# A Strassen step in the projections of five head pairs: 1024 columns as 2x2 blocks with seven block products in four PSUM banks

## The chip, the cores and the metric

The kernel runs on one core of one Trainium2 chip. The metric is the time of one execution on the device in microseconds, and the kernel before takes 841.94 us (median of three runs). Engines are named as the profile names them: PE is the matrix engine, with PEld for its weight loads; DVE is VectorE; ACT is ScalarE; POOL is GpSimd; SP is the engine that issues nearly all transfers.

## The reference, cut to what matters

Two layers on one sequence of 512 tokens and 1024 channels. Each normalises its input, projects it with one wide matrix, mixes tokens by attention, multiplies with a gate, projects back and adds the residual. Layer A has three groups of dilated window attention, so its projection has 10 blocks of 1024 columns: q, k and v for each of three groups, and the gate.

```python
def mixer_a(hn, w_in, w_out, q_gain, k_gain, t5_bias):
    proj = hn @ w_in                                  # (512, 1024) @ (1024, 10240)
    n_qkv = N_DIL_GROUPS * 3 * BRANCH_WIDTH
    qkv = proj[..., :n_qkv].reshape(b, s, N_DIL_GROUPS, 3, N_HEADS, HEAD_DIM)
    gate = proj[..., n_qkv:]
    for g, (window, dilation) in enumerate(DILATED_PAIRS):
        q = rms_norm(qkv[:, :, g, 0], q_gain[g])
        k = rms_norm(qkv[:, :, g, 1], k_gain[g])
        v = qkv[:, :, g, 2]
        o, lse = dilated_group_attention(q, k, v, t5_bias[...], dilation, reach)
    alpha = jax.nn.softmax(jnp.stack(lses), axis=0)
    y = jnp.sum(alpha[..., None] * jnp.stack(outs), axis=0)
    y = y.reshape(b, s, BRANCH_WIDTH) * jax.nn.silu(gate)
    return y @ w_out
```

Layer B is neighbourhood attention on an 8 x 64 grid, with a projection to 4096 columns; the change leaves its arithmetic alone. All inputs are float32.

## The kernel before, in words

**Split matmuls.** Every large product is made of three matmuls on operands that are split into a rounded part and the rest: h·h, h·l and l·h (`mm3`, L221). The normalised activations are split once, into `hn_h` and `hn_l`. Weights are split as they come: `loads` (L166) and `raws` (L175) bring 128 x 1024 tiles `wraw` by SP (three buffers), and `split` (L128) makes `wh` by a cast on ACT (L132) and `wl` by a subtraction (L138), two of five on POOL and the others on DVE. `wh` and `wl` have four buffers of 512 columns each, a ring that `splits` (L192) keeps three pieces ahead of the matmuls.

**Layer A** goes through eight pairs of heads (`main_a`, L548). A pair projects two blocks of 512 columns (`project_qk`, L451, by `project`, L251: eight k tiles, four token tiles of 128 in four PSUM banks, the activations stationary and the weights moving), and then two blocks of 128 columns, v of the first group (`v0_a`) and the gate (`gate_a`), the other way round (`project_t`, L276). The first block holds k and v of groups 1 and 2 (`rawk`, and `v12` of it), the second q of all groups and k of group 0 (`rawq`). At the eighth k tile each bank is evacuated by ACT with the token's norm as scale (L485); `squares` (L284) then squares on POOL (L288, L290) and sums by head on DVE (L291), and `head_norm` (L297) makes the inverse root and scales on DVE (L313).

**Attention of a pair** runs while the next pair is projected. `rawq` is turned in 32 x 32 blocks on DVE (L574), written to DRAM and read back (`move_q`); k of groups 1 and 2 is transposed on PE and scaled on DVE (L566). Scores come in two halves (`attn_a`, L774), with softmax on DVE and ACT in tile `p`; the weights are turned by DVE (L755) and by way of DRAM (`turner`), and `weigh` (L850) and `put_y` (L681) make the pair's rows of y, split again into `y_h` and `y_l`.

**What sets the order.** PE's order is written out: `run` (L914) takes the steps of `main`, keeps a clock of planned matmul time, and slips in a step of `side` (attention and everything else that is not projection) when its due time on that clock has come. A `yield "wait", key, delay` holds the next side step until a stamp and a delay after it; a guard in `main` forces side steps out until a stamp exists; `later_on` gives jobs a due time. The other engines are ordered by a scheduler ahead of time, except for instructions that are pinned to program order, and each works its queue in order.

Ahead of pair 0, `side` (near L1183) normalises, sums squares for the norm's scales, and loads tables.

## Time and profile before

| what | value |
|---|---|
| time, median of 3 runs | 841.94 us (841.76 to 842.17) |
| time of the profiled execution | 842.18 us |
| its span, first to last instruction | 840.4 us |
| instructions | 15567 |
| DVE, ACT, POOL busy | 515.4, 425.1, 283.5 us |
| HBM read, written | 109.11 MB, 31.12 MB |
| start of pairs 1 to 6 in the span | 64.6, 124.7, 188.6, 252.6, 316.5, 380.4 us |

Busy time counts an instruction from its start to its end, so a wait that an instruction spends after its start is counted as busy. Matmuls are pipelined: their own durations overlap, and the distance of their starts is what one costs. Rows of a group give the count, the busy time and the mean of one in nanoseconds, then the engine's idle time ahead of them and what ended it.

### The profile page before, as it was taken

The page shows a single profiled execution, that of the slowest core. Times are in us where ns is not written, and L with a number is a line of the kernel's source. Part 1 is how long each engine was busy: PE and PEld are TensorE (multiplying, and loading weights), DVE is VectorE, ACT ScalarE, POOL GpSimd, SP SyncE. Part 2 cuts the span into 40 slices and gives each one's busy share as a digit, 9 for nine tenths or more (in the row PEclk, how much of TensorE's full clock was granted, in tenths as well). Part 3 has the DMA queues.
Part 4 walks back from the last instruction along what each step waited for, and adds up shares of the span by engine and source line. Part 5 has one row for each costly group of instructions (what it writes and reads, how often), then busy time and mean ns, then how long its engine had stood idle before and what let it go on. Part 6 is the DMA issues. An engine that isn't in the chain of part 4 may idle for free.

```text
span 840.4 us, 15567 instructions
## 1 busy us (share of the span) xinstructions
PE 833.6 (99%) x5698; PEld 675.0 (80%) x5698; DVE 515.4 (61%) x1355; ACT 425.1 (51%) x893; POOL 283.5 (34%) x432
## 2 busy tenths in 40 slices
PE   9999999999999999999999999999999999999998
PEld 7788888788788788788788787888878877777787
DVE  7355684684584675575574755548456778668653
ACT  7432653553552652652653564345375465663551
POOL 3352442441441432432531341112521625235211
PEclk9999999999999999999999999999999999999999
DMA  7346468478368478387376364165236646457223
GB/s 254 112 122 189 150 194 245 164 215 260 127 186 238 143 222 245 107 228 231 111 221 184 111 195 126 56 231 183 78 98 182 180 142 182 129 151 204 102 94 132
DMA packets 64221, 141.25 MB, mean 168 GB/s; under 512 B 5648, under 2 KB 23248, under 8 KB 64144
## 3 DMA queue, kind: packets, MB, share of 16 engines
q1 hardware_dynamic: 64000, 139.99, 54.6%
q8 instruction: 45, 0.74, 0.4%
q14 instruction: 32, 0.26, 0.1%
q10 hardware_dynamic: 144, 0.26, 0.1%
HBM read 109.11 MB, written 31.12 MB: 167 GB/s over the span
## 4 chain that ended last, share of the span: by engine, by line
PE 93%; ACT 3%; DVE 2%; issue 1%; DMA 1%; POOL 0%; SPq 0%; DVEq 0%; ACTq 0%
PE acc L215 79%; PE o L215 5%; PE log L215 5%; PE tp L219 3%; ACT p L1101 1%; ACT p L679 1%; DVE hn_l L403 1%; DMA wraw<-in_w 1%; ACT wh L132 0%; DVE raw L313 0%; DVE p L1091 0%; ACT raw L485 0%; DVE pt L999 0%; DVE wl L138 0%; PE pa L215 0%
## 5 line engine op out<-in xcount | busy, mean ns | idle before, releaser
L132 ACT CAST wh<-wraw 128x512 fp32r<-128x512 f32 (+1 forms) x259 | 158.4, 613 | 288.8 <-PE acc L215 236.7
L215 PE MATMUL acc<-wh,hn_h 128*128 128x512 f32 x704 | 281.9, 401 | 1.3 <-ACT hn_h L402 0.7
L215 PE MATMUL acc<-wl,hn_h 128*128 128x512 f32 x704 | 274.1, 390 | 0.3 <-POOL wl L138 0.3
L215 PE MATMUL acc<-wh,hn_l 128*128 128x512 f32 x704 | 274.3, 390 | 0.0
L138 POOL TENSOR_TENSOR wl<-wraw,wh 128x512 fp32r<-128x512 f32 (+1 forms) x104 | 135.5, 1302 | 362.6 <-ACT wh L132 337.9
L138 DVE TENSOR_TENSOR wl<-wraw,wh 128x512 fp32r<-128x512 f32 (+1 forms) x156 | 114.2, 732 | 148.7 <-ACT wh L132 148.0
L215 PEld LDWEIGHTS acc<-wh,hn_h 128*128 128x128 f32 x704 | 132.1, 188 | 35.5 <-issue 5.6
L215 PEld LDWEIGHTS acc<-wh,hn_l 128*128 128x128 f32 x704 | 132.1, 188 | 28.6
L215 PEld LDWEIGHTS acc<-wl,hn_h 128*128 128x128 f32 x704 | 132.4, 188 | 25.9 <-POOL wl L138 0.8
L215 PE MATMUL acc<-y,wh 128*128 128x512 f32 (+1 forms) x272 | 82.4, 386 | 0.0
L215 PE MATMUL acc<-hn_h,wh 128*128 128x512 f32 x192 | 76.1, 397 | 0.8 <-ACT rawk L485 0.6
L215 PE MATMUL acc<-hn_h,wl 128*128 128x512 f32 x192 | 74.9, 390 | 0.0
L215 PE MATMUL acc<-hn_l,wh 128*128 128x512 f32 x192 | 74.8, 390 | 0.0
L679 ACT ACTIVATE p<-p,mn 128x512 f32<-128x512 f32 (+3 forms) x128 | 69.3, 585 | 0.7 <-DVE mn L678 0.2
L291 DVE TENSOR_REDUCE ss<-sq 128x4 f32<-128x256 f32 (+1 forms) x96 | 48.5, 505 | 28.1 <-POOL sq L290 18.3
L839 ACT ACTIVATE p<-p,mn 128x512 f32<-128x512 f32 (+1 forms) x64 | 44.9, 702 | 38.5 <-DVE mn L828 38.5
L755 DVE STREAM_TRANSPOSE tr<-p 128x512 f32<-128x512 f32 (+1 forms) x80 | 53.6, 684 | 9.3 <-ACT p L679 8.7
L215 PEld LDWEIGHTS acc<-y,wh 128*128 128x128 f32 x272 | 48.3, 189 | 9.6 <-issue 1.3
L215 PE MATMUL acc<-y,wl 128*128 128x512 f32 (+1 forms) x136 | 51.5, 379 | 0.0
L215 PEld LDWEIGHTS acc<-hn_h,wh 128*128 128x128 f32 x192 | 36.0, 188 | 9.2 <-ACT rawk L485 1.0
L215 PEld LDWEIGHTS acc<-hn_h,wl 128*128 128x128 f32 x192 | 36.0, 188 | 7.7
L215 PEld LDWEIGHTS acc<-hn_l,wh 128*128 128x128 f32 x192 | 36.1, 188 | 7.1
(128 smaller groups left out, 965.6 us busy)
## 6 DMA issues: line engine op xcount, KB each, us to landing
wraw<-in_w SPq DMA_DIRECT2D x119, 512.0 KB
td<-tr SPq DMA_DIRECT2D x14, 1024.0 KB
pt<-td SPq DMA_DIRECT2D x56, 256.0 KB
qd<-rawq SPq DMA_DIRECT2D x6, 1024.0 KB
qt<-qd SPq DMA_DIRECT2D x24, 256.0 KB
td<-tr SPq DMA_DIRECT2D x6, 896.0 KB
pt<-td SPq DMA_DIRECT2D x24, 224.0 KB
e<-l_d SPq DMA_DIRECT2D x32, 112.0 KB
```

Source lines behind the costliest of these rows:

```text
L132: nc.scalar.copy(h, raw)
L138: eng.tensor_sub(l, raw, h.bitcast(F32))
L215: nc.tensor.matmul(o, l, r, **kw)
L219: nc.tensor.transpose(o, i, ident)
L291: nc.vector.tensor_reduce(ss[:, i * ns : (i + 1) * ns], sq.rearrange("p (a b) -> p a b", b=64), axis=AX.X, op=ALU.add)
L403: return nc.vector.scalar_tensor_tensor(l, xk, g, h.bitcast(F32), op0=ALU.mult, op1=ALU.subtract)
L679: nc.scalar.activation(pr, pr, AF.Copy, scale=mn[:, 3:4])
L755: nc.vector.transpose(dst, src[:, :n].rearrange("p (i b k) -> p i b k", b=4, k=32))
L839: nc.scalar.activation(row, row, AF.Exp, bias=mn[:, 1:2], scale=-1.0, accum_out=mn[:, 2:3])
L1101: nc.scalar.activation(pr[:, o : o + n], pr[:, o : o + n], AF.Exp, bias=mn[:, 0:1], scale=-1.0, accum_out=mn[:, 2:3])
```

## The change

In pairs 1 to 5 the two blocks of 512 columns become one product of 2x2 blocks: tokens in two halves of 256, k in two halves of four tiles, columns in the two blocks of 512. `seven` (new) makes seven block products of 4 k tiles x 2 token tiles instead of eight. The stationary side of each is a block of hn or one of four forms (sums and differences of hn's blocks, split again), which `make_forms` makes once ahead of pair 0's bias tables, from whole hn tiles that `join` adds up on POOL. The moving side is a weight block or a sum of weight blocks: `sums` (new) brings the four blocks and adds them up in place on POOL, eight additions of 128 x 1024 a pair, and gives 14 tiles (28 pieces of 512) to the split, with a set of its own for which go to POOL. Products are accumulated in four PSUM banks in such an order that a bank is read once in the middle and once at the end: a column block's result is the sum of two readings, the first by ACT into SBUF, the second by DVE on top (`first`, `second`), or one reading.

With it go these moves. Squares of the five pairs go to ACT. The scaling of k12 goes from DVE to ACT. The copy of v's first 64 elements goes from POOL to ACT. The split of y for pairs 0 to 3 is put off to pair 6, since `y_l` of these shares memory with forms. The columns of the q block are permuted in DRAM for pairs 0 to 5. `wraw` has five buffers instead of three, and two tiles `wsum` are added; the bias tables `e0` and `e12`, `eg`, and `gt` have one buffer fewer, layer B's tiles borrowing others; `v12` has two places instead of three. Due times and guards of the side steps are set anew for the five pairs. Layer B and pairs 0, 6 and 7 compute as before.

```diff
+SEVEN = range(1, 6)
+SPLIT_LATER = range(0, 4)
...
+    def split(raw, n, to_pool=None):
...
-        to_pool = turn[0] * pool[0] % pool[1] < pool[0]
+        if to_pool is None:
+            to_pool = turn[0] * pool[0] % pool[1] < pool[0]
...
+            if hc in SEVEN:
+                yield b, None, None
+            else:
+                yield from ((b + 512 * KT * (i ^ first), 512, KT) for i in range(2))
...
+    def load(src, n, own=False):
+        if own:
+            raw = wp.tile([P, 1024], F32, tag="wsum", name="wsum", bufs=2)
+        else:
+            raw = wp.tile([P, 1024], F32, tag="wraw", name="wraw", bufs=5)
+        dst = raw[:, : src.shape[1]]
...
+        nc.sync.dma_start(dst, src)
...
+    def add(a, b):
+        nc.gpsimd.tensor_add(a, a, b)
+
+    def sums(off):
+
+        at = lambda n, k: w[:, off + 512 * (KT * n + k) : off + 512 * (KT * n + k + 2)]
+        js = range(2)
+        acc, x, y, z = {}, {}, {}, {}
+        for j in js:
+            acc[j] = load(at(0, 2 * j), 512, True)
+            yield acc[j], None, (1,) if j == 0 else ()
+        for j in js:
+            x[j] = load(at(1, 2 * j), 512)
+            yield acc[j], partial(add, acc[j], x[j]), ()
+        for j in js:
+            y[j] = load(at(1, 4 + 2 * j), 512)
+            yield acc[j], partial(add, acc[j], y[j]), ()
+        for j in js:
+            yield y[j], None, (1,) if j == 0 else ()
+        for j in js:
+            yield x[j], partial(add, x[j], y[j]), (1,)
+        for j in js:
+            z[j] = load(at(0, 4 + 2 * j), 512)
+            yield z[j], None, (1,) if j == 0 else ()
+        for j in js:
+            yield acc[j], partial(add, acc[j], z[j]), (1,) if j == 1 else ()
+
     def loads():
         for off, n, ks in blocks():
+            if n is None:
+                for raw, job, to_pool in sums(off):
+                    yield raw, 1024, 512, job, to_pool
+                continue
...
+    def ahead(source, n):
         queue = []
-        for src, cols, n in loads():
-            raw = wp.tile([P, 1024], F32, tag="wraw", name="wraw", bufs=3)
...
+        for item in source:
+            queue.append(item)
+            if len(queue) > n:
                 yield queue.pop(0)
         yield from queue
...
+    def summed():
+        for raw, cols, n, job, to_pool in ahead(loads(), 1):
+            if job:
+                job()
+            yield raw, cols, n, to_pool
+
+    def pieces():
+        for raw, cols, n, to_pool in ahead(summed(), 1):
...
+                pool = None if to_pool is None else c // step in to_pool
+                yield (*split(raw[:, c : c + step], step, pool), min(n, step))
+
+    def splits():
+        return ahead(pieces(), 3)
...
                 yield
 
+    def seven(hc):
+
+        ys, xs = ([ps_acc.tile([P, 512], F32, tag="acc", name="acc") for _ in range(2)] for _ in range(2))
+        part_of = lambda t, k0, i0: lambda k, i: t[:, k0 + k, P * (i0 + i) : P * (i0 + i) + P]
+        whole = lambda k0, i0: (part_of(hn_h, k0, i0), part_of(hn_l, k0, i0))
+        form = lambda n: tuple(part_of(t, 0, 0) for t in st["forms"][n])
+        q = wk.tile([P, 2048], F32, tag="rawq", name="rawq", bufs=1).rearrange("p (c i r) -> p c i r", c=16, i=4)
+        raw, st["v12", hc] = part(hc % 2), part(2 + hc % 2)
+        k_to = lambda i: sb(rk, 1024 * (hc % 2) + 256 * i, [[2048, 2], [1, 256]])
+        q_to = lambda i: q[:, :, i, :]
+        k_of = lambda t: t.rearrange("p (n c) -> p n c", n=2)
+        q_of = lambda t: t.rearrange("p (c r) -> p c r", c=16)
+        kss, qss = (wk.tile([P, 32], F32, tag="ss", name="ss") for _ in range(2))
+        first = lambda to, of, s, o: lambda i, t: nc.scalar.activation(
+            to(o + i), of(t), AF.Copy, scale=s[:, o + i : o + i + 1]
+        )
+        second = lambda to, of, s, o: lambda i, t: nc.vector.scalar_tensor_tensor(
+            to(o + i), of(t), s[:, o + i : o + i + 1], to(o + i), op0=ALU.mult, op1=ALU.add
+        )
+
+        def with_squares(put, of_k, o):
+            def both(i, t):
+                put(i, t)
+                if of_k:
+                    squares(raw[:, o + i, :], kss, o + i, 4, True)
+                else:
+                    squares(q[:, :, o + i, :], qss, o + i, 8, True)
+            return both
+
+        products = (
+            (xs, whole(0, 0), True, first(k_to, k_of, rs_n, 0)),
+            (ys, form(0), True, first(q_to, q_of, rs_neg, 2)),
+            (xs, form(1), False, first(q_to, q_of, rs_neg, 0)),
+            (ys, form(3), False, with_squares(second(q_to, q_of, rs_neg, 0), False, 0)),
+            (xs, form(2), False, with_squares(second(q_to, q_of, rs_neg, 2), False, 2)),
+            (ys, whole(4, 0), True, with_squares(second(k_to, k_of, rs_n, 0), True, 0)),
+            (xs, whole(4, 2), False, with_squares(first(k_to, k_of, rs_n, 2), True, 2)),
+        )
+        stamp["seven", hc, -1] = clock[0]
+        for n, (acc, stat, start, evac) in enumerate(products):
+            hls = {}
+            order = [(k, i) for k in range(4) for i in range(2)]
+            if n == 0:
+                order = [(0, 0), (1, 0), (0, 1), (1, 1)] + order[4:]
+            for k, i in order:
+                if k not in hls:
+                    chore(True)
+                    hls[k] = next(wsteps)
+                if k == 3 and i == 0 and n < 2:
+                    yield (("weighed", hc - 2), ("q", hc - 1))[n]
+                mm3(acc[i], stat[0](k, i), stat[1](k, i), *hls[k], start and k == 0, k == 3, skip_group_check=not start)
+                if k == 3:
+                    evac(i, acc[i])
+                yield
+            stamp["seven", hc, n] = clock[0]
+            if n == 4:
+                normed(q, qss, 8, "rawq", hc)
+        normed(raw, kss, 4, "rawk", hc)
...
+        if act:
+            nc.scalar.activation(wide, v, AF.Square)
+        else:
+            nc.gpsimd.tensor_mul(wide, v, v)
...
+    rk = wk.tile([P, 4096], F32, tag="rawk", name="rawk", bufs=1)
+    sx = big.tile([P, 4, 4, 256], F32R, name="sx")
+    st["yf"] = big.tile([P, 4, S], F32, name="yf")
...
+        late = 5000 if hc in SEVEN else 9000
+        head_norm(raw, ss, ns, False, late if key == "rawk" and 0 < hc < NHC - 1 else 0)
...
+        yield "gt", hc - 2
+        gt = wk.tile([P, S], F32, tag="gt", name="gt", bufs=2)
+        eg = wk.tile([P, S], F32, tag="eg", name="eg", bufs=1)
...
+        if hc in SEVEN:
+            nc.scalar.copy(vt[:, 0:64], vt[:, EXT - 64 : EXT])
...
+        stamp["pair", hc] = clock[0]
+        if hc == SEVEN[-1] + 1:
+            for n in SPLIT_LATER:
+                later_on(4000 + 7000 * n, partial(split_y, n))
+        if hc in SEVEN:
+            yield from seven(hc)
+        else:
+            yield from chain(*(parts[::-1] if hc == NHC - 1 else parts))
...
+        if hc in SEVEN:
+            yield "wait", ("pair", hc + 1), 9500
...
-            nc.vector.tensor_scalar(k12[:, g, :], tp, gk[:, g + 1 : g + 2], None, op0=ALU.mult)
+            scaled(k12[:, g, :], tp, g + 1)
...
+        yield "wait", ("rawq", hc), 13500 if hc in SEVEN else 18000 if moved(hc) else 13000 if hc < NHC - 1 else 23500
...
+            if hc + 1 in SEVEN:
+                yield "wait", ("pair", hc + 1), 12500 if hc else 17000
...
+            yield "wait", ("pair", hc + 1), 7000
...
+        if permuted and hc in SPLIT_LATER:
+            dst = st["yf"][:, hc, :].rearrange("p (x ja t) -> p t ja x", t=4, ja=8)
+            of = lambda t: t.rearrange("p (t ja x) -> p t ja x", t=4, ja=8)
+            tc.keep_in_program_order(nc.vector.tensor_mul(dst, of(gt), of(o)))
+            stamp["gt", hc] = 0
+            return
...
+    def split_y(hc):
+
+        h, l, y = st["y_h"][hc], st["y_l"][hc], st["yf"][:, hc, :]
+        pin(nc.scalar.copy(h, y))
+        pin(nc.gpsimd.tensor_sub(l, y, h.bitcast(F32)))
+        stamp["ya", hc, "y"] = 0
+
+    whole = pq.rearrange("p (k t) -> p k t", k=KT)
+    pin = tc.keep_in_program_order
+
+    def join(k):
+        pin(nc.gpsimd.tensor_add(whole[:, k, :], hn_h[:, k, :].bitcast(F32), hn_l[:, k, :].bitcast(F32)))
+
+    def make_forms():
+
+        y_h = st["y"][:, : KT * S].rearrange("p (n m k t) -> p n m k t", n=2, m=2, k=4)
+        st["forms"] = forms = [(y_h[:, n, 0], y_h[:, n, 1]) for n in range(2)] + [
+            (sx[:, 2 * n], sx[:, 2 * n + 1]) for n in range(2)
+        ]
+        a11, a21, a12, a22 = (whole[:, k : k + 4, t : t + 256] for k in (0, 4) for t in (0, 256))
+        f = wk.tile([P, 2, 4, 256], F32, tag="tr", name="form", bufs=1)
+
+        def cut(n, v):
+            h, l = forms[n]
+            pin(nc.scalar.copy(h, v))
+            pin(nc.vector.tensor_sub(l, v, h.bitcast(F32)))
+
+        def less(o, a, b):
+            pin(nc.vector.scalar_tensor_tensor(o, a, -1.0, b, op0=ALU.mult, op1=ALU.subtract))
+
+        pin(nc.gpsimd.tensor_sub(f[:, 0], a22, a21))
+        yield 1500
+        less(f[:, 1], f[:, 0], a11)
+        yield 1500
+        cut(0, f[:, 0])
+        yield 2000
+        less(f[:, 0], f[:, 1], a12)
+        yield 1500
+        cut(1, f[:, 1])
+        yield 2000
+        pin(nc.gpsimd.tensor_sub(f[:, 1], a11, a21))
+        cut(3, f[:, 0])
+        yield 2000
+        cut(2, f[:, 1])
+        yield 2000
+
...
+                    if hc + 1 in SEVEN:
+                        yield "wait", ("pair", hc + 1), (14500 if u == 0 else 25500) if hc else (19500 if u == 0 else 29000)
...
+            later_on(7000, lambda: st.__setitem__(("e", hc + 1), bias_a(hc + 1, True)))
+
+            def finish():
+                put_y(hc, weigh(), True, False)
+                stamp["weighed", hc] = 0
+
+            pending.append(finish)
...
+    def weigh_a(hc):
+        yield "wait", ("pair", hc + 1), 3200 if hc > 1 else 4800
+        pending.pop(0)()
+        yield
...
-            if hc == 1:
-                later_on(20000, lambda: st.__setitem__(("e", 1), bias_a(1, True)))
-            elif hc:
-                st["e", hc] = bias_a(hc)
...
+        join(0)
...
+            join(k)
...
+        st["y"] = big.tile([P, 12 * S], F32R, tag="y", name="y")
+        y = st["y"].rearrange("p (k t) -> p k t", t=S)
+        low = sx.rearrange("p a b c -> p (a b c)")
+        st["y_h"] = [y[:, k, :] for k in range(KT)]
+        st["y_l"] = [low[:, S * k : S * k + S] for k in range(4)] + [y[:, KT + k, :] for k in range(4)]
         yield 2500
+        yield from make_forms()
...
+        nc.gpsimd.tensor_scalar(rs_neg, rs_n, -1.0, None, op0=ALU.mult)
...
+                if hc in SEVEN:
+                    yield from chain(q_a(hc), weigh_a(hc), v_a(hc), k_a(hc))
+                else:
+                    yield from chain(k_a(hc), q_a(hc), v_a(hc))
```

In the lines left out, `y_h` and `y_l` become lists of slices, `project`'s uses of them follow, layer B takes the changed tiles, and `attn_a` takes new due times.

135 lines of the change are left out of this document (61 added, 74 removed).

## The prediction

> **What bounds the kernel now.** I read the page's first part, the chain of waits in order of time, PE's own waits, and then busy time pair by pair.
>
> ```profile
> span 840.4 us, 15567 instructions
> ...
> PE 833.6 (99%) x5698; PEld 675.0 (80%) x5698; DVE 515.4 (61%) x1355; ACT 425.1 (51%) x893; POOL 283.5 (34%) x432
> ```
> ```profile
> 302.56 23.17 PE acc L215 x102
> ```
> ```profile
> PE acc L215 <- ACT hn_h L402: 0.7, 1, 0.7
> ```
> TensorE is busy for all but some 7 us. The second row is one piece of the chain: 102 projection matmuls in 23.17 us with nothing between them, 0.2272 us each from start to start. The third is PE's longest wait inside the work. So the time is the number of 128x512 matmuls, as long as the other engines keep up. The profiled execution took 842.18 us, 1.8 us more than its span and 0.2 us above the median of 841.94.
>
> The next view cuts the five pairs that change into windows (start of one pair to start of the next); columns are the window's length and each engine's busy time. The last row is the same for projection matmuls alone in one of them.
>
> ```profile
> core 0: us, PE busy (x) PEld busy (x) DVE busy (x) ACT busy (x) POOL busy (x), PEclk, DMA share, GB/s
> 64.60:124.70 60.10, 60.10 (x445) 49.27 (x444) 37.80 (x100) 30.57 (x60) 22.02 (x35) 1.00 0.60 180
> 124.70:188.60 63.90, 63.90 (x493) 51.99 (x492) 39.55 (x97) 31.67 (x61) 25.25 (x40) 1.00 0.69 206
> 188.60:252.60 64.00, 64.00 (x494) 52.02 (x494) 39.06 (x99) 32.02 (x61) 22.87 (x36) 1.00 0.59 189
> 252.60:316.50 63.90, 63.90 (x493) 51.98 (x492) 39.69 (x99) 31.65 (x61) 22.77 (x36) 1.00 0.68 200
> 316.50:380.40 63.90, 63.90 (x493) 52.00 (x492) 39.90 (x99) 31.90 (x61) 22.75 (x36) 1.00 0.66 193
> sum 315.80, PE 315.80 PEld 257.26 DVE 196.01 ACT 157.81 POOL 115.66; mean PE 63.16 PEld 51.45 DVE 39.20 ACT 31.56 POOL 23.13
> ```
> A pair takes 63.16 us, all of it PE; in it DVE works 39.20, ACT 31.56 and POOL 23.13 us. The clock is 1.00 throughout.
>
> **TensorE: what is removed.** A pair's 1024 columns cost 2 blocks x 8 k x 4 token tiles x 3 = 192 matmuls. Seven products of 4 k x 2 tiles x 3 cost 168. 24 x 0.2272 = 5.45 us a pair, 27.3 us in five pairs. If nothing else is late, a pair takes 63.16 - 5.45 = 57.71 us.
>
> The Trainium skill, page "TensorE: Matmul & The Clock Gate", section "Back-to-back issue gap", gives some 131 ns for a 128x512 matmul in a sustained stream of weight loads and matmuls, and so speaks for a smaller gain: 120 x 0.131 = 15.7 us by its figure, an estimate. The trace's 0.2272 us is for the same thing, and decides.
>
> **The other engines' bill.** Rows by form (count | busy, mean ns), then the split line alone in the five pairs (min/median/max):
>
> ```profile
> L132 ACT CAST wh<-wraw 128x512 fp32r<-128x512 f32 x243 | 150.2, 619 | 272.5 <-PE acc L215 222.2 <-DMA wraw<-in_w 29.7 <-issue 6.0
> L288 POOL TENSOR_TENSOR sq<-rawq 128x512 f32<-128x512 f32 x24 | 25.5, 1083 | 6.3 <-ACT rawq L485 5.1 <-issue 1.3
> L485 ACT ACTIVATE rawq<-acc,rs_n 128x512 f32<-128x512 f32 x32 | 21.7, 688 | 0.4
> L485 ACT ACTIVATE rawk<-acc,rs_n 128x256 f32<-128x256 f32 x56 | 21.2, 489 | 0.3
> L290 POOL TENSOR_TENSOR sq<-rawk 128x256 f32<-128x256 f32 x32 | 19.5, 613 | 17.8 <-ACT rawk L485 16.5
> L566 DVE TENSOR_SCALAR k<-tp,gk 128x512 f32<-128x512 f32 x16 | 11.5, 730 | 1.1 <-PE tp L219 1.1
> L138 POOL TENSOR_TENSOR wl<-wraw,wh 128x384 fp32r<-128x384 f32 x7 | 7.1, 1014 | 45.5 <-ACT wh L132 45.5
> L1056 DVE SCALAR_TENSOR_TENSOR qkb<-tp,gk,qkb 128x512 fp32r<-128x512 f32 x8 | 6.0, 752 | 11.2 <-ACT qkb L652 11.2
> L652 ACT ACTIVATE qkb<-tp,gk 128x512 fp32r<-128x512 f32 x8 | 5.5, 685 | 5.3 <-PE tp L219 5.3
> ```
> ```profile
> L138 DVE TENSOR_TENSOR wl<-wraw,wh x60: 646/684/1509, 67.8 to 376.0; 128x512 fp32r<-128x512 f32 x60
> ...
> L138 POOL TENSOR_TENSOR wl<-wraw,wh x40: 1282/1289/1649, 68.5 to 378.6; 128x512 fp32r<-128x512 f32 x40
> ```
>
> *Splits.* Each weight piece is cast by ACT (wh) and its rest (wl) made by DVE or POOL. Today a pair has 20 pieces, 12 on DVE and 8 on POOL. Seven products need 28 pieces instead of 16, and the diff puts 6 of these on POOL; with the 4 pieces of v0 and gate (two in five on POOL) that is 24.4 on DVE, 7.6 on POOL, 32 on ACT. DVE +12.4 x 0.684 = +8.48; ACT +12 x 0.619 = +7.43; POOL -0.4 x 1.289 = -0.5 us.
>
> *Evacuation.* Today 4 of 0.688 and 8 of 0.489 on ACT, 6.66 us. Then 8 on ACT, 5.50 us, and 6 `scalar_tensor_tensor` from PSUM on DVE. Nearest row is L1056, also from PSUM with a second SBUF operand, 0.752: +4.51 us.
>
> *Squares* leave POOL (4 x 1.083 + 4 x 0.613 = 6.78) for ACT; no row shows them there, but 4 x 0.688 + 4 x 0.489 = 4.71 us, the rows of the same shapes. The two k scalings leave DVE (-1.46) for ACT (+1.37).
>
> *Sums.* Eight 128x1024 additions a pair on POOL. From 384 to 512 elements L138 on POOL grows by (1.289 - 1.014)/128 = 2.15 ns an element, which gives 2.39 us at 1024; from 256 to 512 the squares grow by 1.84 ns, which gives 2.02. I take 2.39, from the row with two different inputs: +19.1 us.
>
> Per pair: ACT 31.56 + 7.43 - 1.16 + 4.71 + 1.37 = 43.9; POOL 23.13 - 0.5 - 6.78 + 19.1 = 34.9; DVE 39.20 + 8.48 + 4.51 - 1.46 = 50.7, all under 57.7. By busy time alone PE stays the bound, with DVE at 88%.
>
> **What busy time leaves out.** Two stretches, DVE's instructions and then POOL's beside them (start, duration):
>
> ```profile
> 307.82 0.69 DVE L291 TENSOR_REDUCE ss<-sq 128x8 f32<-128x512 f32 x1 [0.31 <-POOL sq L288]
> 309.20 1.40 DVE L138 TENSOR_TENSOR wl<-wraw,wh 128x512 fp32r<-128x512 f32 x1 [0.69 <-ACT wh L132]
> ...
> 314.30 0.19 DVE L120 SCALAR_TENSOR_TENSOR rs<-na,rs 128x32 f32<-128x32 f32 x1
> ...
> 314.75 1.27 DVE L119 SCALAR_TENSOR_TENSOR na<-na,nv 128x32 f32<-128x32 f32 x1
> ```
> ```profile
> 307.75 1.30 POOL L138 TENSOR_TENSOR wl<-wraw,wh 128x512 fp32r<-128x512 f32 x1
> 309.00 1.05 POOL L288 TENSOR_TENSOR sq<-rawq 128x512 f32<-128x512 f32 x1
> ...
> 314.68 1.29 POOL L138 TENSOR_TENSOR wl<-wraw,wh 128x512 fp32r<-128x512 f32 x1 [1.81 <-ACT wh L132]
> ```
> A DVE instruction with two SBUF operands that starts while POOL reads SBUF lasts until POOL is done, and its own time more: 1.40 for 0.684, 1.27 for 0.19. The reduction at 307.82, with one operand, is not held. The delay was 0.72 of a 1.05 us instruction and 1.08 of a 1.29. The median split took 0.684, so most are spared today. The sums are nearly twice as long, eight a pair, and each stands between the split of the block it overwrites and the split of what it makes, just where DVE wants to split the other half. Bounds: none delays DVE (0), or each holds it in full, 8 x 2.39 = 19.1 us. I take half, 1.2 us each, between the splits spared and the two held: 9.6 us. DVE then needs 50.7 + 9.6 = 60.3 us, more than PE's 57.7, and the pair takes 60.3: 2.6 us given back, 13.0 in five pairs.
>
> **Start, queues, buffers.** The forms of hn (8 sums, 2 differences on POOL; 6 more steps on DVE and 4 casts) are made in pair 0:
>
> ```profile
> 0.00:64.60 64.60, 62.64 (x277) 50.37 (x278) 36.86 (x77) 33.45 (x62) 25.19 (x41) 1.00 0.50 163
> ```
> Each other engine idles 27 us or more there. 8 x 1.289 + 2 x 2.39 = 15.1 us on POOL and 6 x (2 x 0.684) = 8.2 on DVE fit; the steps push the bias tables' and the scales' matmuls back by 12.5 us of planned time, against a guard on the scales in the second block's last k. Between 0 and 2 us; I take 1.0.
>
> ```profile
> ACT wh L132 <- PE acc L215: 236.7, 128, 4.4
> ```
> ```profile
> SPq L184 <- DVE wl L138: 301.2, 81, 11.8
> ```
> Casts wait for PE to free a ring buffer and weight loads for splits, so loads (as many and as large as before) have slack: 0. But `z`'s second load waits on SP for `x`'s split, and the transfers of attention stand behind it in the queue. PSUM's four banks leave a product 24 x 0.2272 = 5.45 us until its bank is written again; two evacuations of 0.752 fit unless DVE is over 3.9 us late, and then PE stops. The deferred splits of y go to pair 6, and the single bias buffers rely on loads issued after the previous pair's last scores: 0 each, and a landing per pair if that cover fails.
>
> Sum: 842.2 - 27.3 + 13.0 + 1.0 = 828.9; 0.2 less for the median, **828.7 us**.
>
> **Rivals.**
> (1) *The sums hold DVE for most of their length.* For: both held instructions lost 0.72/1.05 and 1.08/1.29, 76% on average; DVE's queue is in order, so a held split also holds softmax and evacuations. Against: the median split is spared. At 76%, 14.5 us, DVE needs 65.2: 2.0 more than today's 63.16 in each pair, 842.2 + 10.2 + 1.0 - 0.2 = 853.2, slower. It decides from (63.16 - 50.7)/8 = 1.56 us a sum, 65%.
> The Trainium skill, page "SBUF — State Buffer", section "Who interferes with whom", states it as a rule: a Vector instruction with two SBUF inputs and a GpSimd one that reads SBUF take one shared read port exclusively, and the later fully blocks. The two held rows agree, and so does the reduction that was not.
> (2) *The sums hide.* If the queue's order puts single-operand work beside them, PE alone sets the pair: 842.2 - 27.3 + 1.0 - 0.2 = 815.7.
> (3) *The ring is too short.* Four pieces fed PE for 4 x 12 x 0.2272 = 10.9 us; now 5.45.
> ```profile
> 252.60:316.50 63.90, 0.00 (x0) 0.00 (x0) 11.43 (x24) 10.88 (x24) 0.53 (x4) 1.00 0.68 200
> ```
> This is the windows view for tile p: softmax holds DVE for 11.43 us a pair, 5.7 in each half. If a half goes ahead of the 4 splits due in it, 5.7 + 4 x 0.684 - 5.45 = 3.0 us of PE are lost. With hidden sums that is 815.7 + 15 = 830.7 for one half a pair, 845.7 for both.
>
> **Chances.** Forecast 0.45, (1) 0.28, (2) 0.15, (3) 0.12. About 0.2% (1.7 us) is what a measurement here can tell. Faster: 0.45 + 0.15 + half of (3), 0.66; same: 0.02 each from (1) and (3) at their edges, 0.04; slower: 0.26 + 0.04 = 0.30. The range goes from (2), 815, to a little past (1), 856. The forecast's own, with sums holding DVE for 40% to 60% of their length (7.6 to 11.5 us a pair), is 819 to 838.
>
> **What would show it.** Block matmuls fall from 704 to 664 in each of the three rows of acc, those named for the forms counted in; DVE busy in a pair near 60 of 60 us with splits well above 684; POOL 35; sums at 2.0 to 2.4 us; PE waits on wl, some 2 to 3 us a pair. Splits near 684 and pairs of 57.7 mean (2); PE dry behind softmax means (3); pairs over 63.2 with splits of 1.4 and more mean (1). It is also wrong if evacuations in two steps, the forms or an SP transfer stop PE for more than a microsecond a pair.

## The result: slower, 897.3 against 842.0 us

The changed kernel takes 897.33 us (median of 4 runs, 895.89 to 900.33), the kernel before 842.0 us on the same chip: ratio 1.0662, 95% interval 1.0635 to 1.0689. The forecast was 828.7. The profiled execution took 897.23 us. The page's span and its first part:

```profile
span 895.4 us, 15558 instructions
...
PE 839.4 (94%) x5578; PEld 665.6 (74%) x5578; DVE 617.3 (69%) x1437; ACT 481.7 (54%) x998; POOL 370.0 (41%) x436
```

PE runs 120 matmuls less and is busy 5.8 us longer; it was busy 99% of the span and is now at 94%. The windows of pairs 0 to 6, each from its first projection matmul to the next pair's, to within 0.2 us:

```profile
core 0: us, PE busy (x) PEld busy (x) DVE busy (x) ACT busy (x) POOL busy (x), PEclk, DMA share, GB/s
0.00:73.90 73.90, 66.87 (x272) 53.16 (x273) 53.07 (x73) 37.19 (x67) 49.89 (x54) 0.95 0.46 160
73.90:147.50 73.60, 61.75 (x420) 47.96 (x418) 59.81 (x126) 40.79 (x79) 32.64 (x33) 0.91 0.50 154
147.50:219.30 71.80, 62.94 (x469) 48.90 (x468) 57.41 (x115) 41.26 (x79) 32.48 (x28) 0.95 0.68 195
219.30:287.90 68.60, 62.47 (x470) 48.38 (x469) 54.47 (x112) 40.33 (x77) 31.64 (x31) 0.98 0.52 155
287.90:359.60 71.70, 63.93 (x469) 48.98 (x468) 58.55 (x117) 41.02 (x80) 36.48 (x37) 0.95 0.59 178
359.60:432.40 72.80, 65.18 (x470) 50.17 (x469) 56.09 (x115) 42.07 (x81) 35.30 (x39) 0.93 0.55 164
432.40:494.30 61.90, 59.74 (x478) 48.20 (x477) 30.12 (x79) 34.52 (x67) 29.27 (x44) 1.00 0.53 164
```

Pair 0 grew from 64.6 to 73.9 us, pairs 1 to 5 from 315.8 to 358.5, pair 6 from 58.5 to 61.9; what follows is 0.4 shorter. That is the whole difference of 55.0 us in span. In pairs 1 to 5 the window less PE's busy time is 42.2 us; it was zero. The granted clock, 1.00 in every one of them before, is 0.91 to 0.98: one minus the clock times the length adds up to 20.3 us. The stretches at half clock last 41.0 us, and PE stands still in 6.5 of them, so some 3 of the 20.3 are among the stops already. The 70.0 us between 27.3 saved and 42.7 lost are then 42.2 of stopped PE, some 17 of half clock while PE works, and a rest of some 11 in which matmuls start further apart, which the view counts as busy. No engine is full: DVE works 57.3 us of a mean 71.7, where the forecast had it at 60.3 of 60.3.

PE's waits, whole span (the longest of before inside the work was 0.7 us):

```profile
PE acc L265 <- DVE wl L141: 13.0, 9, 4.1
PE o L265 <- DMA pt<-td: 12.0, 4, 5.3
PE acc L265 <- POOL wl L141: 7.0, 17, 0.9
PE tp L269 <- DVE rawk L427: 6.3, 3, 3.6
PE acc L265 <- ACT rawq L601: 5.7, 2, 5.5
PE acc L265 <- ACT wh L134: 3.8, 3, 3.0
```

Not one cause: weights split late (rows 1, 3, 6), attention's transfers late (2), k late (4), and in pair 0 an evacuation that stood in ACT's queue (5). The groups that the forecast sized:

```profile
L141 DVE TENSOR_TENSOR wl<-wraw,wh 128x512 fp32r<-128x512 f32 (+1 forms) x148 | 112.2, 764 | 93.4 <-ACT wh L134 93.0
L141 DVE TENSOR_TENSOR wl<-wsum,wh 128x512 fp32r<-128x512 f32 x70 | 72.6, 1056 | 35.0 <-ACT wh L134 35.0
L190 POOL TENSOR_TENSOR wsum<-wsum,wraw 128x1024 f32<-128x1024 f32 x30 | 74.3, 2475 | 53.9 <-DVE wl L141 30.0
```

Splits of summed weights take 1.056 us in the mean against 0.764 for the others. Two stretches of pair 3, POOL's and then DVE's beside it (start, duration, and in brackets the idle time before):

```profile
216.86 2.40 POOL L190 TENSOR_TENSOR wsum<-wsum,wraw 128x1024 f32<-128x1024 f32 x1
219.22 0.65 POOL L125 TENSOR_SCALAR na<-na 128x16 f32<-128x16 f32 x1
219.84 2.39 POOL L190 TENSOR_TENSOR wraw<-wraw 128x1024 f32<-128x1024 f32 x1
222.20 0.66 POOL L126 TENSOR_TENSOR rs<-rs,na 128x16 f32<-128x16 f32 x1
222.86 2.77 POOL L190 TENSOR_TENSOR wsum<-wsum,wraw 128x1024 f32<-128x1024 f32 x1
225.59 0.40 POOL L119 TENSOR_TENSOR na<-rs 128x16 f32<-128x16 f32 x1
```
```profile
220.22 2.56 DVE L141 TENSOR_TENSOR wl<-wsum,wh 128x512 fp32r<-128x512 f32 x1 [0.41 <-ACT wh L134]
...
234.28 1.43 DVE L427 TENSOR_TENSOR rawk<-rawk,rs 128x256 f32<-128x256 f32 x4 [1.59 <-POOL rs L126]
```

Two things are seen. A split that starts at 220.22, inside a sum that ends at 222.23, lasts 2.56 us instead of some 0.68: the hold that the prediction spoke of. And k's reciprocal root, a chain of small dependent steps on POOL (L114 to L126), has a sum of 2.4 us or more ahead of five of its steps (three are shown), so `rawk` is scaled only at 234.28; PE had stopped for it at 231.12.

### The profile page after: what moved, and what is told of

It is laid out like the page before. It is cut to its first block, busy times and chain, and to the rows that moved or that the text cites. A ratio compares the mean times of both kernels' runs of the same rounds, so it can differ in the third digit from the quotient of the medians.

```text
span 895.4 us, 15558 instructions
## 1 busy us (share of the span) xinstructions
PE 839.4 (94%) x5578; PEld 665.6 (74%) x5578; DVE 617.3 (69%) x1437; ACT 481.7 (54%) x998; POOL 370.0 (41%) x436
## 4 chain that ended last, share of the span: by engine, by line
PE 58%; DVE 16%; DMA 9%; ACT 9%; issue 4%; POOL 3%; SPq 0%; ACTq 0%; DVEq 0%; POOLq 0%
PE acc L265 47%; PE o L265 5%; DVE wl L141 4%; PE tp L269 3%; DMA pt<-td 3%; PE log L265 2%; DMA wsum<-in_w 2%; ACT p L1028 2%; ACT wh L134 2%; DMA wraw<-in_w 2%; ACT p L815 2%; DVE ss L407 2%; DMA td<-tr 1%; POOL wl L141 1%; DVE rawq L427 1%
## 5 line engine op out<-in xcount | busy, mean ns | idle before, releaser
L265 PE MATMUL acc<-wh,hn_h 128*128 128x512 f32 x504 | 204.6, 407 | 5.0 <-ACT wh L134 3.8
L265 PE MATMUL acc<-wl,hn_h 128*128 128x512 f32 x504 | 199.5, 397 | 6.7 <-DVE wl L141 4.6
L265 PE MATMUL acc<-wh,hn_l 128*128 128x512 f32 x504 | 198.3, 395 | 0.0
L265 PEld LDWEIGHTS acc<-wh,hn_h 128*128 128x128 f32 x504 | 95.8, 190 | 31.9 <-ACT wh L134 5.5
L265 PEld LDWEIGHTS acc<-wl,hn_h 128*128 128x128 f32 x504 | 96.0, 191 | 29.7 <-DVE wl L141 7.2
L141 DVE TENSOR_TENSOR wl<-wsum,wh 128x512 fp32r<-128x512 f32 x70 | 72.6, 1056 | 35.0 <-ACT wh L134 35.0
L190 POOL TENSOR_TENSOR wsum<-wsum,wraw 128x1024 f32<-128x1024 f32 x30 | 74.3, 2475 | 53.9 <-DVE wl L141 30.0
L134 ACT CAST wh<-wsum 128x512 fp32r<-128x512 f32 x80 | 48.6, 616 | 72.3 <-PE acc L265 37.1
L265 PE MATMUL acc<-wh,y 128*128 128x512 f32 x160 | 57.6, 424 | 0.0
L265 PE MATMUL acc<-wh,sx 128*128 128x512 f32 x160 | 52.2, 396 | 0.1
```

The source lines that it names most:

```text
L134: nc.scalar.copy(h, raw)
L141: eng.tensor_sub(l, raw, h.bitcast(F32))
L190: nc.gpsimd.tensor_add(a, a, b)
L265: nc.tensor.matmul(o, l, r, **kw)
```

## The experiments

The theories. **A**: the sums hold DVE through the shared read. **B**: the ring of four split pieces feeds PE only 5.45 us, so any lateness of a split reaches it. **C**: attention's transfers are late for `weigh`, for their place in SP's queue. **D** (formed on the way): k's root on POOL is late because the sums stand between its steps. All lengths of pairs are between first projection matmuls, from the trace; the kernel before took 842.0 to 843.4 us beside every run.

### The sums alone

*e1_no_sums*: the four jobs are dropped.

```diff
-            yield acc[j], partial(add, acc[j], x[j]), ()
+            yield acc[j], None, ()
```


> The changed kernel without its eight additions a pair on POOL; loads, splits, matmuls and evacuations stay, so the weights are wrong. Theory A, the sums hold two-operand DVE instructions and that starves PE: DVE's splits go back to about 0.69 us, pairs 1 to 5 from 71.7 to about 60 us, the whole to 838 to 848 (pair 0 stays 9 us long). Theory B, DVE's queue is in order, puts scaling, transposes and softmax ahead of splits, and the ring of pieces covers only 5.45 us: PE still waits for splits, pairs stay at 66 to 70 us, the whole at 870 to 888. Theory C, the long stops are the reads of attention's turned weights (pt from td) landing late: stops ahead of tile o stay at some 3 us a pair, half-clock stretches stay.

*e2_write_only*: GpSimd writes as long as it would have added, and reads nothing.

```diff
-        nc.gpsimd.tensor_add(a, a, b)
+        nc.gpsimd.memset(a, 0.0)
+        nc.gpsimd.memset(a, 0.0)
+        nc.gpsimd.memset(a[:, :512], 0.0)
```


> Each addition on POOL is replaced by three memsets of the same tile (1024, 1024 and 512 elements, about 2.3 us together, no SBUF read), so the weights are zero where a sum was; order and dependences are those of the changed kernel. Theory A, by the shared read of SBUF: DVE's splits at about 0.69 us though POOL is busy as long, the whole within 10 us of the kernel without sums. Rival, the sum's length in the chain load - sum - cast - rest is what starves PE: the whole at 885 to 897.

*e8_half_sums*: each sum in two halves of 512 columns, all else as in the changed kernel.


> Each 128x1024 addition on GpSimd becomes two of 128x512: the same work, half the length of one hold. Theory A, held for the rest of one instruction (VectorE's instruction that starts in a sum waits for that sum's end only): VectorE's held time falls from 9 to 12 us a pair to 5 to 7, pairs 1 to 5 shorten by 2 to 4 us each, time 878 to 890. Rival: the next half starts before VectorE gets in, or the total length of the sums decides: held time and pairs as they were, time 893 to 900. Theory B or C alone: no change.

*e10_dve_sums*: `nc.vector.tensor_add` in place of `nc.gpsimd.tensor_add`.


> The changed kernel with its eight additions of a pair on VectorE instead of GpSimd; nothing is left out. In the changed kernel VectorE's instructions on 128x1024 with two SBUF operands took 1.22 us, so 9.8 us of work a pair come to VectorE, and the sums' holds go. Theory A in its narrow form (only the hold matters, and it costs 9 to 12 us of VectorE a pair): work replaces hold, time 890 to 900. Theory A in its wide form (the chain load, sum of 2.45 us, cast, rest is late by the sums' length on GpSimd as well): 2 to 4 us a pair are won, 878 to 888. If VectorE was not what made PE wait: over 900.

| run | us | ratio to before, 95% |
|---|---|---|
| e1_no_sums | 875.0 | 1.0379 (1.0349 to 1.0409) |
| e2_write_only | 883.3 | 1.0477 (1.0417 to 1.0538) |
| e8_half_sums | 906.8 | 1.0754 (1.0730 to 1.0778) |
| e10_dve_sums | 885.0 | 1.0505 (1.0475 to 1.0535) |

Without sums 22.3 us go, and 875 is still 33 above before: the sums are a real part and not the main one. Of the 22.3, 14.0 (897.3 - 883.3) go when GpSimd only writes, and the holds with them (by the measure below from 11.0 to some 3 us a pair); 8.3 stay. Neither is a clean price: an instruction that only writes does not wait for the second operand's load, and in e2_write_only PE waits 25.2 us for splits on POOL, 7.0 in the changed kernel. On DVE a sum takes 1.224 us in the median against 2.398 on GpSimd, 9.8 us of work a pair; the time by which DVE's instructions exceed the usual length (lower quartile) of their own form falls from 11.0 to 2.7 us a pair, and 12.3 us of the time go. So the sums on DVE cost more than no sums and less than the sums on GpSimd, which hold DVE and stand in POOL's queue as well. Halving missed: the holds fell to 9.5 us a pair, but the stops before `tp` rose from 6.3 to some 17 us. That pointed at k's chain (D).

### One repair at a time

*e3_no_forms*: `form` gives plain blocks, and `join` and `make_forms` are dropped.


> The changed kernel without the making of forms (no joins, differences or casts in pair 0); products 1 to 4 use blocks of hn in their place, so their values are wrong; all else stays. If pair 0's loss of 9.3 us (5.5 us of PE waiting for an evacuation of rawq that stands behind a form's cast in ACT's queue, and the half clock after it) comes from the forms alone: pair 0 back to 64.6 to 65.5 us and the whole at 887 to 889. If the new due times or buffers cause it: 895 to 898.

*e4_pace*: the reads of `pt` follow one another sooner, ahead of the write of `qd`.

```diff
-... 8500, 1200)
+... 8500, 600)
```


> The four reads that bring pt back are spaced 0.6 us instead of 1.2 us in the plan, so in SyncE's queue all of them now stand ahead of the write of qd, which waits for VectorE's transposes of rawq; nothing else changes by design. Theory A (the sums hold VectorE through the shared SBUF path; the late reads are a consequence): the stops of PE before the tile o shrink by less than 3 us in total, time 892 to 898. Theory C (the queue's order makes the reads late): the read that left at 289.31 us leaves some 3.5 us earlier, the o stops of 13.7 us in pairs 2 to 6 fall under 4 us together with one half-clock stretch, time 879 to 888. Theory B (the ring of weight pieces is too short): no change of the hn_h,wl stops, so at most C's gain.

*e7_late_cast*:

```diff
-        cut(2, f[:, 1])
-        yield 2000
+        later_on(12000, partial(cut, 2, f[:, 1]))
```


> The last form's cast and rest are issued 12 us of planned time later, so that ScalarE's evacuation of pair 0's rawq stands ahead of the cast that waited 5.47 us for GpSimd. If the queue of ScalarE is what stopped PE at 54.97 us, the stop of 5.5 us and the half-clock stretch behind it (6.83 us long) go, pair 0 falls from 73.9 to 64 to 66 us, time 887 to 890. If GpSimd's late work itself is the cause (its rsqrt chain, slowed by VectorE), another stop of 3 us or more takes its place in pair 0 or at the start of pair 1, time 892 to 898.

*e19_rs_dve*: k's root in pairs 1 to 5 on `nc.vector`.


> The changed kernel with the reciprocal root of k in pairs 1 to 5 on VectorE instead of GpSimd (11 small instructions of about 0.19 us, some 2.2 us a pair), nothing left out. Theory D (k's chain is late because its steps stand between sums in GpSimd's queue): the stops before tp of 6.3 us in all and the half clock behind them go, 2 to 4 us a pair in pairs 3 and 5, time 886 to 893. Theory A by holds alone: two more us of work and more instructions to hold on VectorE, time 897 to 906.

Each took away its stop, wholly or in the main, and hardly moved the time: 900.8 (ratio 1.0684, 1.0604 to 1.0764), 895.4 (1.0638, 1.0614 to 1.0662), 898.4 (1.0654, 1.0631 to 1.0678) and 893.8 us (1.0602, 1.0580 to 1.0624). Without forms pair 0 is back at 64.4 us, and pair 2 has a stop of 9.4 before `o`. With early reads the stops before `o` fall from 13.7 to 4.7 us, and those before `tp` rise from 6.3 to 13.0. With the late cast 2.5 of the 5.5 us of pair 0's stop remain, pair 0 falls to 68.7, and pair 1 rises by 6.3 to 79.9, with 9.4 us before `acc<-wl,y`. With the root on DVE the stops before `tp` are gone, and new ones before `acc<-wh,sx` take 5.1 us. PE, freed at one place, arrives earlier at the next thing that is late. A single repair therefore says little of what its stop costs: the expectations that priced a repair by its stop were missed, e19_rs_dve's by 1 us, e4_pace's and e7_late_cast's by 7 or 8, e3_no_forms' by 12.

### From the other side: nothing but the matmuls

*e6_bare*: no sums, no forms, reads early, as described in its expectation.


> The changed kernel without the eight weight additions of a pair and without the forms of hn (the additions and the making of the forms are left out, the products use plain quarters in their place), and with the reads of pt ahead of qd. Splits, evacuation in two steps, two banks per product, deferred y splits and the ring of five pieces stay. If sums (A), forms and queue order (C) were all of the loss, only the matmuls' saving is left: pairs 0 to 6 at 64.6, 57.7 to 58.5, 58.5, time 814 to 820. Theory B (the ring: four pieces feed PE 5.45 us instead of 10.9): pairs stay at 60 to 63 us with stops before acc<-hn_h,wl or acc<-wh,hn_h of 2 to 4 us each and half-clock stretches behind some of them, time 828 to 845.

*e11_bare_ring*: of the 8 KB per partition that the forms no longer need, two more ring places.

```diff
-        h = wp.tile([P, 512], F32R, tag="wh", name="wh", bufs=4)[:, :n]
+        h = wp.tile([P, 512], F32R, tag="wh", name="wh", bufs=6)[:, :n]
...
-        return ahead(pieces(), 3)
+        return ahead(pieces(), 5)
```


> The run without additions and forms (e6_bare), whose freed buffers give the ring of split weight pieces 6 places instead of 4, filled 5 ahead instead of 3. Theory B: the waits of PE before acc<-wl,hn_h, some 3.6 us in pair 4 of e6_bare, fall under 1 us a pair, pairs 1, 3, 4 and 5 come to 58 to 59.5 us, time 838 to 845 (pair 2 keeps its late o, about 20 us with the half clock). Rival: the splits are late because VectorE's queue holds them behind other work, whatever the ring: under 1 us a pair is won, 849 to 854.

e6_bare took 853.5 us (1.0131, 1.0108 to 1.0155), e11_bare_ring 842.35 (0.9998, 0.9984 to 1.0011). At 853.5 e6_bare lies above both of its ranges. The longer ring is worth 11.2 us there, as B said. The windows of e11_bare_ring, pairs 1 to 5, and its first waits:

```profile
65.90:121.50 55.60, 53.98 (x414) 43.88 (x413) 46.47 (x111) 39.42 (x76) 9.96 (x11) 1.00 0.59 176
121.50:197.30 75.80, 63.25 (x470) 51.01 (x469) 50.82 (x118) 40.52 (x79) 19.46 (x39) 0.89 0.69 202
197.30:256.10 58.80, 58.64 (x469) 47.34 (x468) 43.88 (x107) 39.80 (x78) 12.22 (x16) 1.00 0.64 189
256.10:316.70 60.60, 59.05 (x469) 47.40 (x468) 49.35 (x115) 40.43 (x81) 15.69 (x26) 1.00 0.70 206
316.70:377.10 60.40, 59.16 (x470) 47.43 (x469) 54.10 (x124) 39.96 (x80) 18.97 (x35) 1.00 0.66 198
```
```profile
PE o L265 <- DMA qt<-qd: 9.6, 1, 9.6
PE acc L265 <- DVE wl L141: 5.1, 7, 1.7
```

Pair 3 takes 58.8 us, 5.2 less than before: here the matmuls' saving arrives almost whole (5.45). Pair 2 takes 75.8, nearly all of its excess from a stop of 9.6 us before `o`, two of 1.3 and 1.7, and the half clock behind them (0.89 in the mean). So even with neither sums nor forms, and a longer ring, the kernel only draws level.

*e12_bare_v3* (e6_bare with `v12` in three places and `weigh` planned 10 us into the pair) and *e13_bare_both* (that, and a ring of 5).

```diff
-                    yield (("weighed", hc - 2), ("q", hc - 1))[n]
+                    yield (("weighed", hc - 3), ("q", hc - 1))[n]
...
-        yield "wait", ("pair", hc + 1), 3200 if hc > 1 else 4800
+        yield "wait", ("pair", hc + 1), 10000
```


> e6_bare with a third place for v12 (4 KB of the buffers freed), so that weigh need not come before the first product of the pair after next is evacuated; it is planned 10 us into the pair instead of 3.2 (4.8 at first). Theory C (attention's transfers are late for a weigh that the change moved ahead): pair 2 of e6_bare (80.6 us, with 9.9 us before o, 4.9 before acc<-wh,hn_h, and 17 us of half clock) falls to 59 to 63 us, time 832 to 838. If PE in pair 2 waits for something else as well (weights behind the transfers in SyncE's queue): pair 2 at 68 to 75, time 841 to 848.

> e6_bare with the third place of v12 and the later weigh, and with a ring of 5 places filled 4 ahead (as far as the freed buffers go). If ring and weigh are the two causes left, pairs 1 to 5 come to 58 to 60.5 us each without half-clock stretches, and the time to 822 to 832; that PE's saving alone would give is 815.7. If more is left than 835, a further cause is open.

*e14_bare_early*: e11_bare_ring with pair 0's attention planned earlier.

```diff
-... else (19500 if u == 0 else 29000)
+... else (15000 if u == 0 else 25500)
```


> e11_bare_ring with pair 0's attention planned as early in pair 1 as the later pairs' is (q moved 13.5 us after rawq instead of 18, landing at 13.5 instead of 17, the two score halves at 15 and 25.5 instead of 19.5 and 29 us into the pair). Theory C (weigh waits for transfers that start late because pair 0 is planned later, for a pair that was longer): the o stop of 9.6 us and the half-clock stretch behind it go, pair 2 falls from 75.8 to 58.5 to 62, time 825 to 831. Rival (VectorE is late in pair 1 whatever the plan): the stop moves to log or stays before o with over 4 us, time 834 to 842.

They took 855.0 (1.0147, 1.0125 to 1.0169), 851.0 (1.0100, 1.0083 to 1.0117) and 844.5 us (1.0023, 1.0009 to 1.0037): all three times missed, though e14_bare_early's rival, that the stop stays before `o`, came true. In e12_bare_v3 the stop before `o` fell from 9.9 to 3.3 us and pair 2 from 80.6 to 68.5, but pairs 3 to 5 rose from 187.8 to 200.8, with `weigh`'s step moved among other steps. In e14_bare_early the stop before `o` grew to 11.6 us. Its chain of waits (start, duration) tells why:

```profile
112.48 7.99 DMA wsum<-in_w
...
120.55 0.63 ACT wh L134
121.18 0.02 issue
121.21 0.69 DVE wl L141
121.90 2.41 DVE rawq L427 x4
...
127.28 0.63 DVE rawq L704
127.92 0.02 issue
127.93 0.38 SPq L743
...
129.97 6.85 DMA pt<-td
```

The last three reads of `pt` leave SP only after the write of `qd` (L743). That write waits for `rawq` to be turned on DVE, DVE stands in order behind a split, and the split waits for the next pair's weights, whose load landed at 120.47. So in this run a load of weights holds up the attention of an earlier pair; planning the scores earlier moves nothing of this. The changed kernel has the same chain in pair 4, with a load of 12.40 us and a read of 9.07 ahead of `o` at 298.6. In e4_pace, where the reads go first, that stop is gone.

It is not the only chain. In pair 2 of the changed kernel the longest link is the write of the turned weights itself:

```profile
133.19 12.17 DMA td<-tr
...
147.28 8.34 DMA pt<-td
155.62 0.24 issue
155.86 1.17 PE o L265 x17
```

In e11_bare_ring too the four reads left SP at 126.94, just after that write, issued at 118.06, had landed; its row names the read of `qt`, which landed last, though `o` reads `pt`. The kernel before has the same transfers and does not wait for them. SP's rows, and then PE's first `o` of pair 3, which begins at 188.6:

```profile
178.65 0.38 SPq L764 DMA_DIRECT2D td<-tr  x1
...
191.23 1.33 SPq L768 DMA_DIRECT2D pt<-td  x2
```
```profile
213.25 1.97 PE L215 MATMUL o<-pt,rawk 128*64 128x128 f32 x32
```

There `o` begins 24.4 us into each of pairs 2 to 6, and `td`'s write for the second half takes 11.0 to 12.8 us, in the changed kernel 10.2 to 12.3. The change plans `weigh` 3.2 us into the pair (4.8 for the first), because `v12` has two places, and `o` begins at 4.5 to 10.5 us. So C is in the first place that `weigh` was moved some 20 us ahead of transfers that stayed as long as they were; e12_bare_v3, with `weigh` planned at 10 us, has 3.3 us of pair 2's stop left. SP's order and DVE's order in series add to it in single pairs. A kernel without the write of `qd` ahead of the reads in pair 1 was not run; in e11_bare_ring the reads waited for `td`, and not for their place in the queue.

### Sums again, with the longer ring

*e15_sums_ring*: e11_bare_ring with the sums on GpSimd. *e16_dve_sums_ring*: on DVE. *e20_sums_ring_rs*: e15_sums_ring with k's root on DVE.


> e11_bare_ring (no forms, ring of 6, reads of pt early) with the eight additions of a pair back on GpSimd. Theory A as throughput (the holds make VectorE the bound, 51 + 10 us a pair against PE's 58): 2 to 4 us a pair are lost whatever the ring, time 852 to 864. Theory B (with four pieces ahead a hold reached PE, with six it does not): under 1 us a pair, time 842 to 848.

> e15_sums_ring with the additions on VectorE (9.8 us of work a pair). VectorE then has some 60 us of work a pair: as throughput alone 2 us a pair over PE, time 848 to 856. If the hold is worth as much as the work, the same as e15_sums_ring within 3 us; if the sums' length on GpSimd counts as well, 5 us or more below it.

> e15_sums_ring with k's reciprocal root on VectorE. Theory D: the 27.7 us of stops before tp and some 15 us of the half clock go, time 860 to 872, near e16_dve_sums_ring (872.0). Theory A by holds alone: the stops move to acc<-wl,hn_h, time 890 to 905.

They took 904.9 (1.0738, 1.0719 to 1.0757), 872.0 (1.0345, 1.0330 to 1.0360) and 887.8 us (1.0543, 1.0514 to 1.0572). The eight sums of a pair on GpSimd cost 62.5 us here (904.9 - 842.35), far more than either theory gave: with six pieces ahead they still reach PE, against B. PE's first waits in e15_sums_ring, then in e20_sums_ring_rs:

```profile
PE tp L269 <- DVE rawk L427: 27.7, 4, 9.2
PE acc L265 <- DVE wl L141: 21.4, 10, 6.0
PE o L265 <- DMA qt<-qd: 7.6, 1, 7.6
```
```profile
PE acc L265 <- DVE wl L141: 22.3, 10, 5.4
PE tp L269 <- DVE rawk L427: 12.1, 3, 5.4
PE o L265 <- DMA qt<-qd: 9.9, 1, 9.9
```

Taking k's root off GpSimd is worth 17.1 us here and 3.5 in the changed kernel (e19_rs_dve). That shows D, in part: `tp` still waits 12.1, and the time lies between the two that were expected. On DVE, off POOL and its chain, the sums cost 29.6 (872.0 - 842.35). Between e20_sums_ring_rs and e16_dve_sums_ring 15.8 us remain. The holds differ, 14.0 to 23.0 us a pair against 3.8 to 6.0, but so does the work on DVE, and no run separates them. Why the changed kernel loses only 22.3 us by the same sums is not shown; it stops for forms, ring and transfers as well, and stops may coincide.

### Stops by themselves, and all repairs together

*c1_two_stalls*: the kernel before, with PE made to wait in pairs 2 and 4 for a transpose that goes through DVE and a chain of products on GpSimd.

```diff
+        if hc in (2, 4):
+            stall(4 if hc == 2 else 10)
```


> The kernel before with two stops of PE made on purpose: at the start of pair 2 PE transposes a tile that waits for one DVE copy and 4 small multiplications on POOL, at the start of pair 4 one that waits for 10. Theory D, a stop of PE over some 3.5 us also halves the clock for 6.8 us: the first stop (about 2 us) costs its own length, the second (about 5 us) its length and 3.4 us more, in all about 842 + 2.5 + 5 + 3.4 = 853. Without it: 849.5, and the clock stays 1.00 in both pairs.

863.7 us, ratio 1.0244 (1.0206 to 1.0282), where 853 was expected. The stops came out at 7.62 and 9.31 us instead of some 2 and 5, since the chain also stood in those engines' queues. The windows of the first and behind it:

```profile
124.76:132.38 7.62, 0.24 (x2) 0.00 (x0) 6.58 (x11) 1.73 (x3) 2.98 (x5) 0.77 0.57 178
132.38:135.41 3.03, 2.79 (x7) 2.27 (x8) 0.00 (x0) 0.00 (x0) 0.19 (x1) 0.50 1.04 295
135.41:142.00 6.59, 6.59 (x30) 5.44 (x29) 0.69 (x1) 1.25 (x2) 1.28 (x1) 0.98 0.38 98
```

After the stop the clock stays at 0.50 for 3.03 us more, 7 matmuls in place of some 13. The two pairs grew by 9.5 and 11.6 us: a stop costs itself and 1.9 or 2.3 us more. The 20.3 us of half clock in the changed kernel are this answer to stops, in a kernel that had none before.

*e18_valid_ring5*: the changed kernel with sums on DVE, early reads, late cast, ring of 5 with four raw places.


> The changed kernel with nothing left out: additions on VectorE, pt's reads ahead of qd, the last form's cast behind rawq's evacuation, and a ring of 5 split pieces filled 4 ahead, for which the raw weights give up one of their 5 places. e10_dve_sums took 885. If the causes add up, the ring is worth 5 to 8 us, the other two 3 to 8: time 868 to 878. If four raw places make the loads late (stops before acc<-wh): over 885. Below 842 would need every stop gone, which no reading here supports.

888.6 us (1.0544, 1.0522 to 1.0565): the repairs did not add up, a miss. Pair 0 is at 64.0, but pair 1 has 8.3 us before `acc<-wh,sx` and pair 2 13.9 before `o`. e10_dve_sums, with 885.0, stays the best form of the change itself; none beats the kernel before.

## Why the prediction was wrong, step by step

- **Matmuls: right.** Rows for `acc<-wh,hn_h` give 504 and those for the forms 80 + 80 (half of `acc<-wh,y` and of `acc<-wh,sx`, the other half being h·l), together the 664 forecast. Where nothing was late (pair 3 of e11_bare_ring) 5.2 of the 5.45 us a pair arrived.
- **Durations and bills: right or near.** Sums 2.39 us forecast, 2.398 in the median (mean 2.475); ACT, POOL and DVE a pair 43.9, 34.9 and 60.3 forecast, 41.1, 33.7 and 57.3 measured. The holds, forecast at half of each sum (9.6 us), are 11.0, with 3.3 in the kernel before.
- **"DVE then needs 60.3 us, more than PE's 57.7, and the pair takes 60.3": this step failed.** It took a pair's length as the largest of the engines' sums. DVE is not full at 57.3 of 71.7 us; pairs are long because single results are late at the moment PE wants them. The give-back, forecast at 13.0, measures 70.0 in pairs 1 to 5 (42.7 + 27.3).
- **The clock: left out.** The view showed 1.00 throughout, and stops were priced at their length. In pairs 1 to 5 the half clock takes 20.3 us, some 17 of them while PE works. The Trainium skill, page "TensorE: Matmul & The Clock Gate", section "What's actually happening", describes a gate at 4/8 or 8/8 set by activity in a free-running window of 3413 ns; the traces agree on both numbers (0.50, and stretches of 3.41, 6.83 and 10.24 us). Its table puts the fall after at least one idle window; here 2.1 us of idle time within one was enough (last section), and the measurement decides.
- **"Loads, queues: 0" failed.** The prediction named the point (transfers of attention stand behind `z`'s second load) and gave it nothing. The stops before `o` take 13.7 us in pairs 2 to 6; in the bare runs one such stop takes 10 us and the half clock behind it. What the sum put at nothing is that the change moves `weigh` from 24.4 us into the pair to 3.2 while its transfers stay as long; SP's order together with DVE's is shown for pair 4. Pair 6, where the deferred splits of y stood at 0, grew by 3.4 us: 1.9 are such a stop, and the cause of the rest is open.
- **Start, 1.0 us (0 to 2) forecast, 9.3 measured** in pair 0. The last form's difference stood on POOL behind k's root, its cast on ACT waited 5.47 us for it, and `rawq`'s evacuation stood behind the cast (with a later cast pair 0 is 5.2 us shorter, without forms 9.5). Total work fitted, as forecast; the order of the queues did not.
- **Rivals.** (1) had the direction, with 853.2 us, and a mechanism that is some 14 of the 55 us by e2_write_only; it was DVE's bill again. The page "SBUF — State Buffer" of the Trainium skill, section "Who interferes with whom", agrees with e2_write_only, where GpSimd writes without reading and 14.0 us go. (2) did not occur. (3), the ring, is real at 11.2 us between e6_bare and e11_bare_ring, near the 15 given for one half a pair; it was held too unlikely, and taken to exclude the others, while it adds to them. The late k was in no rival.

Between 815.7 and 897.3 stand, each on top of the last: 26.7 for what is late in e11_bare_ring, 11.2 for the ring, 21.5 for the forms and the late reads (e1 against e6), 22.3 for the sums. The order matters (the sums are worth 22.3 or 62.5 us), so these are steps of one ladder, not shares. Open is how much of the 26.7 would go if `weigh` came late enough for its transfers without moving the steps around it.

## What to carry to other kernels

In a kernel where PE never stops, busy times summed by engine show that a change *could* fit and not that it does: follow the results that PE waits for through every queue in series, and count what the change puts ahead of them. A cushion that is halved (5.45 us ahead in place of 10.9) can turn lateness that was free before into stops (11.2 us in the bare kernel), and repairing one stop moves PE on to the next. Long instructions on an engine that also carries a chain of small dependent ones cost the chain their length at every step that they come ahead of, so price them by the chain and not by the engine's idle time. And when a change makes a step come earlier, as `weigh` here, ask what had hidden in the time that it gives up.

## What the runs showed of the hardware that was not expected

All half-clock stretches of a trace begin on one grid of 3.413 us and last 1 to 4 of its steps. Cutting the first 450 us of the changed kernel's and all the experiments' traces into these steps, and adding up PE's idle time in each that was at full clock: with 2.1 us idle or more the next step was at half clock in 89 of 89 cases, with 1.8 to 2.1 in 21 of 33, with 0.6 to 1.8 in 3 of 192. At half clock, 0.6 us idle or more was followed by another step at half clock in 86 of 88. So it needs no whole idle step to lose the clock, and a nearly unbroken one to get it back: a stop of 3.9 us that falls across two steps can cost nothing more (151.98 us in the changed kernel), and one of 2.4 inside a single step costs a stretch.
